# The pool of streamed weights at the upper end of SBUF, everything else 44 KB further down

## Chip, cores and metric

One core of one Trainium2 chip runs the whole program, a single launch. The metric is device time in microseconds, the median of several executions; one further execution is profiled, and all rows below come from it.

## What is computed

Three layers of a language model over 512 positions with a width of 1024, all in float32: an RWKV-7 layer, a layer of forgetting attention, and a layer that mixes sparse attention with a short convolution. Each is followed by an MLP. What takes most of the work are matrix products of activations and weights:

```python
def sq_relu_mlp(h, w_in, w_out):                       # 1024 -> 4096 -> 1024, three times
    return jnp.square(jax.nn.relu(h @ w_in)) @ w_out

def first_block(x, ...):
    for layer in range(DEPTH):                         # layer 0: RWKV-7, layer 1: forgetting attention
        ...
        x = x + rwkv7_time_mix(h, ...)                 # r, k, v, low-rank gates, a recurrence over 512 steps, w_o
        x = x + fox_layer(h, ...)                      # q, k, v projections, attention of 16 heads, w_o
        x = x + sq_relu_mlp(rmsnorm(x, mlp_norm_g[layer]), mlp_w_in[layer], mlp_w_out[layer])

def hybrid_layer(x, ...):                              # the third layer
    proj = xn @ w_in                                   # ... attention, convolution, gates ...
    x = x + mixed @ w_out
    return x + jnp.square(jax.nn.relu(h @ w_up)) @ w_down
```

## The kernel before

Activations lie feature-major: a tile holds 128 features by 512 positions, and eight tiles make a layer's width. To keep float32 accuracy each operand is split into a high part that TensorE reads as `fp32r` and a low part, the remainder: `wh` and `wl` for weights, `xg` and `xgl` (or `hid` and `hidl`, `xk` and `xkl`, and so on) for activations. Each block of 128 by 128 weights takes three matmuls: high with high, low with high, high with low.

Weights are streamed from DRAM by `load_w`: 512 KB at a time into a buffer `wr`, then ScalarE copies each 512 columns into `wh` (L95) and VectorE subtracts to get `wl` (L96). `wh` and `wl` have two buffers of 8 KB per partition each, `wr` three of 4 KB, so the pool `wp` has 44 KB per partition and lives as long as the program.

Two helpers run nearly all projections. `proj_fm` (L150, L151, L153; L156 where the low part is taken late) has a block of weights as the stationary operand, which TensorE loads, and 512 columns of activations as the moving one, which it streams through. `proj_tm` (L272 to L274) has it the other way round: 128 positions of activations stationary, 256 columns of weights moving. The three MLPs, the keys and receptances of the first layer, the convolution and the output projections use `proj_fm`; the values and the projections of the attention layers use `proj_tm`. L1459 to L1461 are the output projection of the first layer, with activations `O` stationary and weights `wo` moving.

What sets the order: every engine runs its instructions in the order that the program was built with, and a buffer is reused when its readers are done. Memory is handed out by pools in two stacks, one from the lower end of SBUF upward and one (`side="right"`) from the upper end downward; a pool starts where the one before it in its stack ends. The lower stack holds constants, `xall` (the residual stream), `wp`, and then the pools of the stage that runs: `net` with `xg` and `xgl`, and on top the pool of the MLP, of the attention and so on. Some of these begin with a block that nothing writes, made by `gap`: 1216 bytes in `fox`, 1728 in `nsa` and the second MLP, 640 in the third. The upper stack is used in the first layer alone: `rwk2` (with `xk`), `rwk1`, `rwk0`, later `rwk3`, `rwk7` and `rwk5`.

Of the kernel before, what the change touches and what calls it, by code (L numbers as in the profile page):

```python
# [31 lines left out]
class Net:  # L32
    def __init__(self, tc, a, ctx):
        self.tc, self.nc, self.a = tc, tc.nc, a
        nc = tc.nc
        nc.scalar.preload_act_table_set("exp_and_others")
        self.ctx = ctx
        self.cp = ctx.enter_context(tc.tile_pool(name="const", bufs=1))
        self.xp = ctx.enter_context(tc.tile_pool(name="xp", bufs=1))
        self.wp = ctx.enter_context(tc.tile_pool(name="wp", bufs=2))  # L40
        self.bs = ctx.enter_context(ExitStack())
        self.uid = 0
        self.nsc = 8
        self.set_banks(3, 2, 2, 1)
        cp = self.cp
        self.vec = cp.tile([P, len(VECS), NK], F32, name="vec")
        nc.sync.dma_start(self.vec, a["vecs"])
        self.ones = cp.tile([P, P], F32, name="ones")
        nc.gpsimd.memset(self.ones, 1.0)
        self.ident = cp.tile([P, P], F32, name="ident")  # L50
        nc.gpsimd.affine_select(self.ident, self.ones, pattern=[[-1, P]], compare_op=ALU.is_equal,
                                fill=0.0, base=0, channel_multiplier=1)
        self.xall = self.xp.tile([P, NK, T], F32, name="xall")
        self.xs = [self.xall[:, m, :] for m in range(NK)]
# [1628 lines left out]
```

## Time and profile before

| | us |
|---|---|
| median of 3 runs (lowest, highest) | 2290.26 (2289.51, 2296.22) |
| the profiled execution, its own time | 2293.3 |
| its span, first to last instruction | 2291.6 |
| TensorE busy | 2195.4 |
| VectorE, ScalarE, GpSimd busy | 1376.9, 937.2, 529.9 |

The first layer takes about the first 500 us of the span, the first MLP runs to about 840, forgetting attention to about 1090, the second MLP to about 1430, the third layer to about 1940 and the third MLP to the end. TensorE's record of a matmul lasts longer than the distance to the next one, since matmuls are pipelined; so the distance between the starts of two neighbours, called pitch below, says more than the length of one. The granted clock of a stretch is given as a share of the full 2.4 GHz.

### The profile page before, as it was taken

The page shows a single profiled execution, that of the slowest core. Times are in us where ns is not written, and L with a number is a line of the kernel's source. Part 1 is how long each engine was busy: PE and PEld are TensorE (multiplying, and loading weights), DVE is VectorE, ACT ScalarE, POOL GpSimd, SP SyncE. Part 2 cuts the span into 40 slices and gives each one's busy share as a digit, 9 for nine tenths or more (in the row PEclk, how much of TensorE's full clock was granted, in tenths as well). Part 3 has the DMA queues.
Part 4 walks back from the last instruction along what each step waited for, and adds up shares of the span by engine and source line. Part 5 has one row for each costly group of instructions (what it writes and reads, how often), then busy time and mean ns, then how long its engine had stood idle before and what let it go on. Part 6 is the DMA issues. An engine that isn't in the chain of part 4 may idle for free.

```text
span 2291.6 us, 32348 instructions
## 1 busy us (share of the span) xinstructions
PE 2195.4 (96%) x12161; PEld 1833.8 (80%) x12161; DVE 1376.9 (60%) x2750; ACT 937.2 (41%) x1920; POOL 529.9 (23%) x631
## 2 busy tenths in 40 slices
PE   4988868999999999999999999999999999999999
PEld 3768767878888889998788888898777788888887
DVE  8998778765444457776744444756665445444444
ACT  5575435433323345665523323344444333332331
POOL 5645211211121112444220120303331112012010
PEclk9999978999999999999999999999999999999999
DMA  3148634213322323332332223232223433223222
GB/s 121 42 136 253 187 85 137 93 48 102 101 92 92 105 98 103 102 101 72 108 101 100 92 92 108 78 111 84 90 85 107 134 111 111 92 93 105 97 92 83
DMA packets 104011, 237.32 MB, mean 104 GB/s; under 512 B 9664, under 2 KB 42176, under 8 KB 103856
## 3 DMA queue, kind: packets, MB, share of 16 engines
q1 hardware_dynamic: 82736, 220.58, 30.3%
q10 hardware_dynamic: 21120, 14.68, 2.1%
q8 instruction: 96, 1.57, 0.3%
q14 instruction: 59, 0.48, 0.1%
HBM read 210.02 MB, written 18.91 MB: 100 GB/s over the span
## 4 chain that ended last, share of the span: by engine, by line
PE 83%; DVE 9%; DMA 3%; ACT 2%; issue 1%; POOL 1%; SPq 0%; ACTq 0%; DVEq 0%; POOLq 0%
PE psacc L150 21%; PE psacc L151 21%; PE psacc L153 20%; PE psacc L272 2%; PE psacc L274 2%; PE psacc L273 2%; PE pso L384 2%; PE pst L374 1%; DVE wl L96 1%; DVE mix L1011 1%; DVE xgl L180 1%; PE pso L1459 1%; PE pso L1460 1%; PE pso L1461 1%; PE pso L1360 1%
## 5 line engine op out<-in xcount | busy, mean ns | idle before, releaser
L95 ACT CAST wh<-wr 128x512 fp32r<-128x512 f32 (+1 forms) x593 | 323.5, 616 | 448.4 <-PE psacc L153 322.6
L96 DVE TENSOR_TENSOR wl<-wr,wh 128x512 fp32r<-128x512 f32 (+1 forms) x581 | 421.8, 779 | 29.1 <-ACT wh L95 26.2
L153 PE MATMUL psacc<-xgl,wh 128*128 128x512 f32 x1104 | 431.7, 392 | 1.5 <-DVE xgl L180 1.5
L150 PE MATMUL psacc<-xg,wh 128*128 128x512 f32 x1104 | 432.6, 392 | 0.0
L151 PE MATMUL psacc<-xg,wl 128*128 128x512 f32 x1104 | 432.1, 391 | 0.0
L150 PE MATMUL psacc<-hid,wh 128*128 128x512 f32 x768 | 297.0, 389 | 0.0
L153 PE MATMUL psacc<-hidl,wh 128*128 128x512 f32 x768 | 297.0, 389 | 0.0
L151 PE MATMUL psacc<-hid,wl 128*128 128x512 f32 x768 | 296.8, 389 | 0.0
L260 POOL TENSOR_TENSOR xall<-xall,yt 128x512 f32<-128x512 f32 x72 | 106.9, 1484 | 663.2 <-DVE yt L259 663.2
L153 PEld LDWEIGHTS psacc<-xgl,wh 128*128 128x128 f32 x1104 | 207.3, 188 | 44.9 <-DVE xgl L180 3.0
L151 PEld LDWEIGHTS psacc<-xg,wl 128*128 128x128 f32 x1104 | 207.4, 188 | 42.5 <-issue 0.8
L150 PEld LDWEIGHTS psacc<-xg,wh 128*128 128x128 f32 x1104 | 207.4, 188 | 41.9 <-ACT xg L179 0.2
L259 DVE TENSOR_TENSOR yt<-psacc,rb 128x512 f32<-128x512 f32 x96 | 66.4, 692 | 265.6 <-PE psacc L153 265.6
L247 DVE TENSOR_TENSOR ht<-ht,psacc 128x512 f32<-128x512 f32 x96 | 66.0, 688 | 224.1 <-ACT ht L246 223.9
L246 ACT ACTIVATE ht<-psacc 128x512 f32<-128x512 f32 x96 | 57.4, 597 | 282.0 <-PE psacc L153 281.9
L153 PEld LDWEIGHTS psacc<-hidl,wh 128*128 128x128 f32 x768 | 144.2, 188 | 29.9
L151 PEld LDWEIGHTS psacc<-hid,wl 128*128 128x128 f32 x768 | 144.2, 188 | 29.8
L150 PEld LDWEIGHTS psacc<-hid,wh 128*128 128x128 f32 x768 | 144.2, 188 | 29.8
L272 PE MATMUL psacc<-wh,xg 128*128 128x256 f32 (+2 forms) x504 | 144.6, 287 | 2.6 <-ACT gt L659 1.5
L274 PE MATMUL psacc<-wh,xgl 128*128 128x256 f32 (+2 forms) x504 | 143.8, 286 | 0.6 <-DVE gq L605 0.6
L273 PE MATMUL psacc<-wl,xg 128*128 128x256 f32 (+2 forms) x504 | 143.7, 285 | 0.0
L204 POOL TENSOR_TENSOR ssacc<-ssacc,sq 128x512 f32<-128x512 f32 x35 | 53.0, 1513 | 224.7 <-ACT sq L203 223.8
(492 smaller groups left out, 3976.5 us busy)
## 6 DMA issues: line engine op xcount, KB each, us to landing
wr<-in_mlp_in_dram SPq DMA_DIRECT2D x96, 512.0 KB, 4.2
wr<-in_mlp_out_dram SPq DMA_DIRECT2D x96, 512.0 KB, 4.4
dQ<-q ACTq DMA_DIRECT2D x8, 1024.0 KB, 5.6
wr<-in_w_q_dram SPq DMA_DIRECT2D x12, 512.0 KB, 3.6
xall<-in_x_dram SPq DMA_DIRECT2D x16, 256.0 KB, 3.9
wr<-in_rw_k_dram SPq DMA_DIRECT2D x8, 512.0 KB, 3.5
wr<-in_rw_r_dram SPq DMA_DIRECT2D x8, 512.0 KB, 3.3
wr<-in_rw_v_dram SPq DMA_DIRECT2D x8, 512.0 KB, 4.6
```

What stands on the lines that cost most here:

```text
L95: nc.scalar.copy(h, r)
L96: (eng or nc.vector).tensor_tensor(wl[:rows, b:f], r, h.bitcast(F32), op=ALU.subtract)
L150: nc.tensor.matmul(ps_, wi[0], xh, start=i == 0, stop=False)
L151: nc.tensor.matmul(ps_, wi[1], xh, start=False, stop=False)
L153: nc.tensor.matmul(ps_, wi[0], xl, start=False, stop=i == n - 1)
L246: nc.scalar.activation(t, ps, AF.Relu)
L247: nc.vector.tensor_tensor(t, t, ps, op=ALU.mult)
L259: nc.vector.tensor_tensor(t, ps, r2, op=ALU.mult)
L260: (nc.vector if q == 3 else nc.gpsimd).tensor_tensor(self.xs[m], self.xs[m], t, op=ALU.add)
L272: nc.tensor.matmul(o, xh[:, b], wh, start=kt == 0, stop=False)
L273: nc.tensor.matmul(o, xh[:, b], wl, start=False, stop=False)
L274: nc.tensor.matmul(o, xl[:, b], wh, start=False, stop=kt == NK - 1)
```

## The change

```diff
         nc.scalar.preload_act_table_set("exp_and_others")
+        self.uid = 0
         self.ctx = ctx
         self.cp = ctx.enter_context(tc.tile_pool(name="const", bufs=1))
         self.xp = ctx.enter_context(tc.tile_pool(name="xp", bufs=1))
-        self.wp = ctx.enter_context(tc.tile_pool(name="wp", bufs=2))
+
+        self.gap(ctx.enter_context(tc.tile_pool(name="wpe", bufs=1, side="right")), 96)
+        self.wp = ctx.enter_context(tc.tile_pool(name="wp", bufs=2, side="right"))
         self.bs = ctx.enter_context(ExitStack())
-        self.uid = 0
```

`wp` goes from the lower stack to the upper one, above it a block of 96 bytes that nothing writes. All pools that stood on `wp` in the lower stack start 44 KB (45,056 bytes) lower, and the pools of the upper stack 45,152 bytes lower, since `wp` and the block now lie above them. Where the pools' first buffers lie in the built programs, in bytes of a partition, and the remainder by 256 of the buffers that TensorE reads:

| pool | starts at, before | after | buffers: remainder before, after |
|---|---|---|---|
| `wp` | 19,360 | 184,192 | `wh`, `wl`, `wr`: 160, 128 |
| `net` | 64,416 | 19,360 | `xg`, `xgl`: 160, 160 |
| first MLP | 121,504 | 76,448 | `hid`, `hidl`: 160, 160 |
| `rwk2` | 192,480 | 147,328 | `xk`, `xkl`: 224, 128 |
| `rwk5` | 163,520 | 118,368 | `O` (low part, last two blocks): 192, 96 |
| `rwkx` | 68,000 | 22,944 | `xr`, `xrl`: 160, 160 |

By 2048 bytes `xg` has a remainder of 928 and `hid` one of 672, before and after. `const` and `xp` stay where they are.

## Rows read from the trace of the kernel before

**Rows 1.** The page: busy time, share, instructions; then the chain that ended last.
```profile
PE 2195.4 (96%) x12161; PEld 1833.8 (80%) x12161; DVE 1376.9 (60%) x2750; ACT 937.2 (41%) x1920; POOL 529.9 (23%) x631
...
PE 83%; DVE 9%; DMA 3%; ACT 2%; issue 1%; POOL 1%; SPq 0%; ACTq 0%; DVEq 0%; POOLq 0%
PE psacc L150 21%; PE psacc L151 21%; PE psacc L153 20%; PE psacc L272 2%; PE psacc L274 2%; PE psacc L273 2%; PE pso L384 2%; PE pst L374 1%; DVE wl L96 1%; DVE mix L1011 1%; DVE xgl L180 1%; PE pso L1459 1%; PE pso L1460 1%; PE pso L1461 1%; PE pso L1360 1%
```

**Rows 2.** Stretches: length; busy (count) by PE, PEld, DVE, ACT, POOL; clock, DMA, GB/s.
```profile
600.00:800.00 200.00, 200.00 (x884) 165.62 (x883) 93.64 (x134) 64.44 (x118) 23.75 (x16) 1.00 0.30 96
...
2000.00:2200.00 200.00, 200.00 (x884) 165.58 (x884) 89.61 (x124) 57.14 (x105) 30.05 (x21) 1.00 0.29 97
```

**Rows 3.** Timeline of PE, first MLP: start, duration in us, line, output<-inputs.
```profile
600.21 0.39 PE L150 MATMUL psacc<-xg,wh 128*128 128x512 f32 x1
...
601.57 0.39 PE L150 MATMUL psacc<-xg,wh 128*128 128x512 f32 x1
```

**Rows 4.** Timeline of PE, keys of the first layer, first block.
```profile
38.52 0.40 PE L150 MATMUL psacc<-xk,wh 128*128 128x512 f32 x1
...
39.92 0.40 PE L150 MATMUL psacc<-xk,wh 128*128 128x512 f32 x1
```

**Rows 5.** Timeline of PE, keys of the first layer, last block.
```profile
86.23 0.39 PE L150 MATMUL psacc<-xk,wh 128*128 128x512 f32 x1
...
88.98 0.39 PE L150 MATMUL psacc<-xk,wh 128*128 128x512 f32 x1
```

**Rows 6.** Timeline of PE, output projection of the first layer.
```profile
479.76 0.39 PE L1461 MATMUL pso<-wo,O 128*128 128x512 f32 x1
...
481.16 0.39 PE L1461 MATMUL pso<-wo,O 128*128 128x512 f32 x1
```

**Rows 7.** Timeline of PE, values of the first layer, 256 columns.
```profile
191.39 0.28 PE L274 MATMUL psacc<-wh,xkl 128*128 128x256 f32 x1
...
192.07 0.28 PE L274 MATMUL psacc<-wh,xkl 128*128 128x256 f32 x1
```

**Rows 8.** Timeline of PE, values of the first layer, a later stretch.
```profile
224.74 0.28 PE L272 MATMUL psacc<-wh,xk 128*128 128x256 f32 x1
...
225.68 0.28 PE L274 MATMUL psacc<-wh,xkl 128*128 128x256 f32 x1
```

**Rows 9.** Timeline of PE, projections of the third layer, 256 columns.
```profile
1514.14 0.28 PE L273 MATMUL psacc<-wl,xg 128*128 128x256 f32 x1
...
1515.94 0.28 PE L273 MATMUL psacc<-wl,xg 128*128 128x256 f32 x1
```

**Rows 10.** Timeline of PE, first MLP, just after an interruption.
```profile
517.19 0.40 PE L151 MATMUL psacc<-xg,wl 128*128 128x512 f32 x1
...
519.27 0.39 PE L151 MATMUL psacc<-xg,wl 128*128 128x512 f32 x1
```

**Rows 11.** Instructions of L150 and L272: count, duration min/median/max in ns, first and last start.
```profile
L150 PE MATMUL psacc<-xg,wh x1104: 387/389/500, 498.0 to 2242.6; 128*128 128x512 f32 x184
L150 PE MATMUL psacc<-hid,wh x768: 389/389/476, 544.6 to 2286.1; 128*128 128x512 f32 x192
L150 PE MATMUL psacc<-xr,wh x64: 387/394/793, 97.7 to 161.5; 128*128 128x512 f32 x64
L150 PE MATMUL psacc<-oh,wh x64: 387/390/499, 1040.0 to 1106.0; 128*128 128x512 f32 x64
L150 PE MATMUL psacc<-zh,wh x64: 389/389/395, 1794.2 to 1886.9; 128*128 128x512 f32 x64
L150 PE MATMUL psacc<-mh,wh x64: 389/389/389, 1893.1 to 1935.9; 128*128 128x512 f32 x64
L150 PE MATMUL psacc<-noh,wh x32: 389/389/496, 1805.9 to 1892.4; 128*128 128x512 f32 x32
L272 PE MATMUL psacc<-wh,xg x504: 274/283/399, 849.8 to 1529.5; 128*128 128x256 f32 x149, 128*128 128x272 f32 x10, 128*128 128x280 f32 x9
L272 PE MATMUL psacc<-wh,xk x128: 276/281/469, 165.7 to 252.4; 128*128 128x256 f32 x128
```

## The prediction

> **What bounds the kernel now.** I read first the busy shares and the chain that ended last [rows 1]: TensorE is busy for 2195.4 of 2291.6 us (96%), and 83% of the chain is its own matmuls, most of them the three products of `proj_fm` (L150, L151, L153). So the time is, to a first approximation, the number of matmuls times the pitch from one start to the next. The second view is that pitch. Between 600 and 800 us, and again between 2000 and 2200 us, TensorE is busy without a gap at the full clock (1.00, which is 2.4 GHz) [rows 2]: 884 matmuls in 200 us, which with the 0.39 us that one matmul lasts is 200.39 / 884 = 226.7 ns each. The start times say the same: 600.21 to 601.57 us holds six pitches, 1.36 / 6 = 226.7 ns [rows 3]. 512 columns at 2.4 GHz are 213.3 ns, so each matmul carries 13.4 ns that isn't columns. Nothing waits there for VectorE, ScalarE or a DMA; only the pitch itself can make these stretches shorter or longer.
>
> **What the change moves.** No instruction is added, removed or reordered: the five engines have the same rows in the same order with the same waits (2353 buffers, 18,913 instructions in both). What changes is where buffers lie. I write places as the remainder of the start address by 256 bytes. Streamed weights (`wh`, `wl`, `wr`) go from 160 to 128. The buffers at the lower end (`xg`, `xgl`, `hid`, `hidl`, `oh`, `zh`, `mh`) keep 160, since 44 KB is a multiple of 256. The buffers at the upper end shift by 44 KB and 96 bytes: `xk` goes from 224 to 128. So in nearly all projections the two operands that TensorE reads, the stationary one (weights) and the moving one (activations), start at the same remainder before and 32 bytes apart after.
>
> **Does a remainder cost time?** The trace has pairs of both kinds, and the pitch differs between them at the same shape and the same full clock:
> Equal (160 and 160): 226.7 ns as above [rows 2, 3]. `xg` and `hid` differ by 256 bytes when taken by 2048, and both sit in these stretches, so I take 256 as the length that counts at most.
> 64 bytes apart (moving `xk` 224, stationary `wh` 160): 38.52 to 39.92 us holds six pitches, 1.40 / 6 = 233.3 ns, steady [rows 4]; a later stretch of the same pair, 86.23 to 88.98 us, has twelve, 2.75 / 12 = 229.2 ns, also steady [rows 5].
> 32 bytes apart in one of three (L1461, where `O`'s low part lies at 192 and the moving `wo` at 160, between two at 160 and 160): 479.76 to 481.16 us, six pitches, 1.40 / 6 = 233.3 ns [rows 6].
> Equal, but just after an interruption: 517.19 to 519.27 us, nine pitches, 2.08 / 9 = 231.1 ns [rows 10]; then it falls to 226.7 and stays. So 231 is what the pitch is while the two reads have not fallen into step, and the equal pair falls into a good step after about ten matmuls. The unequal pairs fall into 229.2 or 233.3.
> I read this as two streams of reads out of one memory that hold each other up now and then. That is argued from the pitches, not shown: these stretches also differ in what else runs beside them.
>
> **The sum.** Term 1, projections with weights stationary: L150 has 1104 + 768 + 64 + 64 + 64 + 64 + 32 = 2160 of them with moving operands at 160 [rows 11], and each has two companions (L151 with L153, or with L156 for `xr`), so 6480 matmuls go from equal to 32 bytes apart. Their new pitch isn't in the trace. Lower end of the loss: 32 bytes are nothing, 226.7 ns. Upper end: the worst steady pair, 233.3 ns. The rows show a step of 64 bytes at 229.2 to 233.3 and a mixture with 32 at 233.3; I take 230 ns, halfway between equal and the 64-byte step's worse value, since 32 is half of that distance. About one in ten of these matmuls stands just after an interruption and pays 231 already, so 6480 x 0.9 x 3.3 ns = +19 us (0 to +39).
> Term 2, the 256-column matmuls with weights moving (`proj_tm`, L272 to L274): here the equal pair isn't the good one. Equal, in the attention layers: 1514.14 to 1515.94 us, fifteen pitches, 1.80 / 15 = 120 ns [rows 9]. 64 bytes apart, with `xk` stationary: six pitches in 0.68 us, 113.3 ns [rows 7], or eight in 0.94 us, 117.5 ns [rows 8]. 3 x 504 = 1512 matmuls [rows 11] go from equal to 32 bytes apart; halfway to the middle of 113.3 and 117.5 (115.4) is 117.7, so 1512 x -2.3 ns = -3.5 us (-10 to 0).
> Term 3, the pairs that become equal: the 3 x 128 = 384 matmuls on `xk` in `rwkv_values` [rows 11] would go from about 115.4 to 120 ns, +1.8 us; the 192 of the keys (L150, L151, L156 on `xk`) from about 231 to 226.7, -0.8 us. Together +1 us (-1 to +2).
> Term 4, the other engines: the casts of the weights (L95, L96), VectorE, GpSimd and the loads also see new addresses. All buffers start at multiples of 32 bytes before and after, and in the long stretches TensorE never waits for them [rows 2]; the trace has no pair of placements to price it. I take 0 (-3 to +3); the recurrence of the first layer, where these engines are waited for, is where it would show.
> The sum is +19 - 3.5 + 1 + 0 = +16.5 us. The profiled execution took 2293.3 us (2291.6 span and 1.7 around it), 3.0 us over the median of the three runs, 2290.26; on the median the forecast is 2306.5, rounded 2306. Its own range is 2288 (term 1 costs nothing, the others as taken, -2.5 us) to 2331 (+39 and +2, term 2 nothing).
>
> **Rivals.**
> Nothing happens. What speaks for it: no wait, no instruction, no transfer changes, and the slow pitches that I blame on remainders stand in the interrupted stretches, where a matmul of another kind or shape is never far. Then the time is 2290 (2286 to 2294). The Trainium skill bears on this: "SBUF — State Buffer", section "Who interferes with whom", says that TensorE and ScalarE never wait for anybody at SBUF, and "TensorE: Matmul & The Clock Gate", section "Step-by-step: what each phase is for", that loading the next weights takes no read bandwidth from the running matmul, since TensorE has two read ports. By that rule addresses can't matter and this rival is right. The trace is against it as far as 226.7 and 233.3 ns for one shape at one clock go [rows 3, 4], but shows no cause.
> Faster. The equal pair isn't the floor: a 256-column matmul at 113.3 ns [rows 7] has 6.7 ns beyond its 106.7 ns of columns, where the 512-column one has 13.4. If the new distance of 32 bytes lets the long stretches fall into such a step, their pitch is 213.3 + 6.7 = 220.0 ns and term 1 becomes 6480 x 0.9 x -6.7 = -39 us; with term 2, -42 us: 2248. It decides itself in the first ten matmuls after each interruption: whichever step the reads fall into holds for the rest of the stretch. For it: with 256 columns every unequal pair is faster than the equal one. Against it: no stretch of 512 columns stays under 226.7 ns. A half of it (223 ns) gives 2270.
> The change doesn't do what it says: the buffers do lie where it puts them, and the order is the same, so this has no weight.
>
> **Chances and range.** Slower by the unequal pitch 0.50, of which 0.04 falls within 0.3%; nothing happens 0.17; faster 0.33, of which 0.01 falls within 0.3%. 0.3% (7 us) is about what a measurement of this kernel can tell from no change. So faster 0.32, same 0.22, slower 0.46. Cases of both signs hold much, so the range spans them: 2248 to 2331 with 0.2 left out, half below (220 ns or better in every stretch) and half above (233.3 ns or worse); the likeliest case's own range is 2288 to 2331.
>
> **What would show it.** In the profile after: the start times of L150, L151 and L153 in the middle of the first MLP (600 us), 230 ns apart if I am right, 226.7 if nothing happens, about 220 if it is faster; the same number in all three MLPs. L272 to L274 in the attention layers under 120 ns, on `xk` about 120. The keys' pitch at 38 us, now equal, down from 233.3 to 226.7 after some ten matmuls: this is the cleanest test of the reading, whatever the long stretches do. VectorE, ScalarE and GpSimd times per instruction unchanged within some ns. The forecast is wrong if 32 bytes act unlike half of 64, which no row excludes, or if the pitch hangs on what else reads the memory and not on the pair.

## The result

| | before | after |
|---|---|---|
| median (lowest, highest), us | 2291.89 (2289.51, 2296.22) | 2329.53 (2326.80, 2332.07) |
| executions | 4 | 4 |
| span of the profiled execution, us | 2291.6 | 2326.3 |
| ratio after / before | | 1.016, 95% interval 1.0147 to 1.0174 |

The change makes the kernel 37.6 us slower. The direction is the forecast's and the time lies in its range, at the upper end of the range of its likeliest case (2288 to 2331), but the forecast itself was +16 us, less than half of what came.

The page of the changed kernel (its code stands two lines further down, so L152, L153 and L155 are L150, L151 and L153 of before, and L274 to L276 are L272 to L274), busy time and then the chain, against [rows 1]:

```profile
PE 2230.8 (96%) x12161; PEld 1830.0 (79%) x12161; DVE 1378.4 (59%) x2750; ACT 937.3 (40%) x1920; POOL 531.1 (23%) x631
...
PE 83%; DVE 10%; DMA 3%; ACT 1%; issue 1%; POOL 1%; SPq 0%; ACTq 0%; DVEq 0%; POOLq 0%
PE psacc L152 21%; PE psacc L153 21%; PE psacc L155 21%; PE psacc L274 2%; PE psacc L276 2%; PE psacc L275 2%; PE pso L386 2%; PE pst L376 2%; DVE wl L98 1%; DVE mix L1013 1%; DMA Qe<-dQ 1%; PE pso L1461 1%; PE pso L1462 1%; PE pso L1463 1%; PE pss L1397 0%
```

The counts are the same, VectorE, ScalarE, GpSimd and the loading of weights (PEld) are within 4 us of before, and the chain has the same make-up. Only the matmuls' busy time grew, by 35.4 us (2195.4 to 2230.8), and the span by 34.7.

The stretches of 200 us in the first and the third MLP, columns as in [rows 2]:

```profile
600.00:800.00 200.00, 200.00 (x858) 160.61 (x857) 89.36 (x127) 61.43 (x112) 23.83 (x16) 1.00 0.29 95
2000.00:2200.00 200.00, 200.00 (x860) 160.69 (x859) 88.00 (x126) 59.03 (x108) 25.46 (x18) 1.00 0.29 95
```

TensorE is again busy without a gap at the full clock, and does 858 and 860 matmuls where it did 884: about 233 ns each in place of 226.7. What happened there is not a wait but a longer pitch, the same in both MLPs.

The timeline of TensorE in the changed kernel, six places, each by a first and a last row: the keys of the first layer just after the clock came up and some matmuls later, the values at two places, the first MLP just after an interruption and in its middle, and the projections of the third layer:

```profile
39.96 0.40 PE L153 MATMUL psacc<-xk,wl 128*128 128x512 f32 x1
...
42.04 0.39 PE L152 MATMUL psacc<-xk,wh 128*128 128x512 f32 x1
...
45.22 0.39 PE L153 MATMUL psacc<-xk,wl 128*128 128x512 f32 x1
...
47.26 0.39 PE L153 MATMUL psacc<-xk,wl 128*128 128x512 f32 x1
...
191.87 0.28 PE L274 MATMUL psacc<-wh,xk 128*128 128x256 f32 x1
...
192.59 0.28 PE L274 MATMUL psacc<-wh,xk 128*128 128x256 f32 x1
...
224.03 0.28 PE L276 MATMUL psacc<-wh,xkl 128*128 128x256 f32 x1
...
225.95 0.28 PE L274 MATMUL psacc<-wh,xk 128*128 128x256 f32 x1
...
519.11 0.39 PE L152 MATMUL psacc<-xg,wh 128*128 128x512 f32 x1
...
521.21 0.40 PE L152 MATMUL psacc<-xg,wh 128*128 128x512 f32 x1
...
599.80 0.39 PE L152 MATMUL psacc<-xg,wh 128*128 128x512 f32 x1
...
601.20 0.39 PE L152 MATMUL psacc<-xg,wh 128*128 128x512 f32 x1
...
1531.53 0.28 PE L274 MATMUL psacc<-wh,xg 128*128 128x256 f32 x1
...
1532.95 0.28 PE L274 MATMUL psacc<-wh,xg 128*128 128x256 f32 x1
```

Read by pairs, with the number of pitches between the two rows:

- Keys, now equal (128 and 128): nine pitches in 2.08 us, 231.1 ns, while the pair finds its step, and then nine in 2.04 us, 226.7 ns. Before it stood at 233.3 and, later, 229.2 [rows 4, 5]. The first nine take the 2.08 us that nine took after an interruption before [rows 10].
- Values, now equal: six pitches in 0.72 us and sixteen in 1.92 us, 120.0 ns both; before 113.3 and 117.5 [rows 7, 8].
- First MLP, now 32 bytes apart: nine pitches in 2.10 us just after an interruption, 233.3 ns, and six in 1.40 us in the middle, 233.3 ns; before 231.1 and 226.7 [rows 10, 3]. There is no better step into which this pair falls: in the whole trace no nine pitches of this kind in a row have a mean under 231.7 ns.
- Projections of the third layer, now 32 bytes apart: twelve pitches in 1.42 us, 118.3 ns; before 120 [rows 9].

Since both programs have the same 12,161 matmuls in the same order, the start of the same matmul can be compared in the two traces. By stages (from the first projection of one to that of the next; the first column begins with the first matmul of all, the last ends with the start of the last; us):

| | first layer | first MLP | forgetting attention | second MLP | third layer | third MLP |
|---|---|---|---|---|---|---|
| before | 485.2 | 351.8 | 257.1 | 350.9 | 478.9 | 350.0 |
| after | 486.4 | 360.3 | 255.8 | 360.6 | 485.5 | 359.9 |
| difference | +1.2 | +8.5 | -1.3 | +9.7 | +6.6 | +9.9 |

And by kind, each interval from one start to the next booked on the matmul that begins it, waits and all: the 6480 of term 1, without the very last, +36.7 us (1490.5 to 1527.2), the 1512 of term 2 -2.0 (190.3 to 188.3), values -0.1, keys +0.2, all else -0.2; together +34.6.

### The profile page after: what moved, and what is told of

The parts are those of the page before. It is cut to its first block, busy times and chain, and to the rows that moved or that the text cites. A ratio compares the mean times of both kernels' runs of the same rounds, so it can differ in the third digit from the quotient of the medians.

```text
span 2326.3 us, 32348 instructions
## 1 busy us (share of the span) xinstructions
PE 2230.8 (96%) x12161; PEld 1830.0 (79%) x12161; DVE 1378.4 (59%) x2750; ACT 937.3 (40%) x1920; POOL 531.1 (23%) x631
## 4 chain that ended last, share of the span: by engine, by line
PE 83%; DVE 10%; DMA 3%; ACT 1%; issue 1%; POOL 1%; SPq 0%; ACTq 0%; DVEq 0%; POOLq 0%
PE psacc L152 21%; PE psacc L153 21%; PE psacc L155 21%; PE psacc L274 2%; PE psacc L276 2%; PE psacc L275 2%; PE pso L386 2%; PE pst L376 2%; DVE wl L98 1%; DVE mix L1013 1%; DMA Qe<-dQ 1%; PE pso L1461 1%; PE pso L1462 1%; PE pso L1463 1%; PE pss L1397 0%
## 5 line engine op out<-in xcount | busy, mean ns | idle before, releaser
L152 PE MATMUL psacc<-xg,wh 128*128 128x512 f32 x1104 | 438.3, 397 | 0.0
L153 PE MATMUL psacc<-xg,wl 128*128 128x512 f32 x1104 | 437.8, 397 | 0.0
L155 PE MATMUL psacc<-xgl,wh 128*128 128x512 f32 x1104 | 437.1, 397 | 0.1
L152 PE MATMUL psacc<-hid,wh 128*128 128x512 f32 x768 | 301.6, 395 | 0.0
L155 PE MATMUL psacc<-hidl,wh 128*128 128x512 f32 x768 | 301.6, 395 | 0.0
L153 PE MATMUL psacc<-hid,wl 128*128 128x512 f32 x768 | 301.4, 395 | 0.0
L155 PEld LDWEIGHTS psacc<-xgl,wh 128*128 128x128 f32 x1104 | 207.0, 188 | 49.4 <-DVE xgl L182 1.0
L153 PEld LDWEIGHTS psacc<-xg,wl 128*128 128x128 f32 x1104 | 207.2, 188 | 48.7 <-issue 0.8
L152 PEld LDWEIGHTS psacc<-xg,wh 128*128 128x128 f32 x1104 | 207.2, 188 | 48.1 <-ACT xg L181 0.2
L155 PEld LDWEIGHTS psacc<-hidl,wh 128*128 128x128 f32 x768 | 143.9, 187 | 35.3
L152 PEld LDWEIGHTS psacc<-hid,wh 128*128 128x128 f32 x768 | 144.0, 187 | 35.1
L153 PEld LDWEIGHTS psacc<-hid,wl 128*128 128x128 f32 x768 | 144.0, 187 | 35.0
L274 PE MATMUL psacc<-wh,xg 128*128 128x256 f32 (+2 forms) x504 | 144.0, 286 | 2.6 <-ACT gt L661 1.4
L276 PE MATMUL psacc<-wh,xgl 128*128 128x256 f32 (+2 forms) x504 | 143.1, 284 | 0.6 <-DVE gq L607 0.6
```

Of the source, the lines that this page charges most:

```text
L152: nc.tensor.matmul(ps_, wi[0], xh, start=i == 0, stop=False)
L153: nc.tensor.matmul(ps_, wi[1], xh, start=False, stop=False)
L155: nc.tensor.matmul(ps_, wi[0], xl, start=False, stop=i == n - 1)
L274: nc.tensor.matmul(o, xh[:, b], wh, start=kt == 0, stop=False)
L276: nc.tensor.matmul(o, xl[:, b], wh, start=False, stop=kt == NK - 1)
```

## The experiments

The theory: the distance by 256 bytes between the start addresses of a matmul's stationary and moving operand sets the pitch. Rivals: the place of the weights at the upper end costs something by itself; or the pitch hangs on what else reads the memory at the time.

### The upper end without the distance

```diff
-        self.gap(ctx.enter_context(tc.tile_pool(name="wpe", bufs=1, side="right")), 96)
+        self.gap(ctx.enter_context(tc.tile_pool(name="wpe", bufs=1, side="right")), 64)
```

> The changed kernel with a block of 64 bytes instead of 96 above the weights: weights at the upper end as in the change, but at a remainder of 160 like the activations. Theory A (the distance by 256 of the two operands' start addresses sets the pitch): 226.7 ns in the long stretches, 2288 to 2293 us, as before the change. Theory B (the place counts: weights at the upper end, far from the activations): 233.3 ns and 2327 to 2332 us, as after the change.

Measured: 2293.83 us against 2292.68, ratio 1.0007 (0.9996 to 1.0017). The stretch from 600 to 800 us of this kernel:

```profile
600.00:800.00 200.00, 200.00 (x884) 165.60 (x883) 91.30 (x130) 62.53 (x114) 23.78 (x16) 1.00 0.30 98
```

884 matmuls again. 32 bytes less above the pool give the whole loss back, so neither the upper end nor the move of everything else by 44 KB costs anything that can be told.

### The distance without the upper end

```diff
+        self.uid = 0
+        self.gap(ctx.enter_context(tc.tile_pool(name="wpe", bufs=1)), 224)
         self.wp = ctx.enter_context(tc.tile_pool(name="wp", bufs=2))
+        self.gap(ctx.enter_context(tc.tile_pool(name="wpf", bufs=1)), 32)
```

> The kernel before, weights in the lower stack as ever, with an unwritten block of 224 bytes ahead of them and one of 32 behind: weights at a remainder of 128, all that stands on them 256 bytes higher and so at 160 as before, the upper stack untouched. Theory A: 233.3 ns in the long stretches and 2326 to 2334 us. Theory B: 226.7 ns and 2288 to 2293 us.

Measured: 2327.97 us, ratio 1.0155 (1.0137 to 1.0172). The same stretch:

```profile
600.00:800.00 200.00, 200.00 (x858) 160.61 (x858) 89.26 (x127) 61.40 (x112) 23.83 (x16) 1.00 0.29 95
```

The kernel before, with its weights 32 bytes off and nothing else of the change, loses what the change loses. The two runs together settle which part of the change acts.

### Other distances

The changed kernel with no block above the pool (stationary operand 64 bytes after the moving one), and with 128 bytes (64 bytes before it):

```diff
-        self.gap(ctx.enter_context(tc.tile_pool(name="wpe", bufs=1, side="right")), 96)
```

> The changed kernel without the block of 96 bytes: weights at a remainder of 224, 64 bytes above the activations' 160. Theory A: slower than before the change, long stretches at 229 to 234 ns (233.3 or 229.2 are the settled values that a 64-byte distance had in the kernel before), 2303 to 2332 us; the attention projections of 256 columns at 113 to 118 ns. Theory B: as after the change, 2327 to 2332 us, with 120 ns.

```diff
-        self.gap(ctx.enter_context(tc.tile_pool(name="wpe", bufs=1, side="right")), 96)
+        self.gap(ctx.enter_context(tc.tile_pool(name="wpe", bufs=1, side="right")), 128)
```

> The changed kernel with 128 bytes instead of 96 above the pool of weights: weights at a remainder of 96, activations of the long stretches at 160, so the stationary operand lies 64 bytes before the moving one. Theory (the distance of the pair by 256 bytes sets the pitch, as in the series of matmuls alone): 229 ns there, so 6480 matmuls go from a mean of 227.25 to about 229.2 (+13 us), the attention layers' 256-column matmuls get a distance of +64 (117.8 ns, -2.6 us): 2302 us, ratio 1.0045. Rival, that any unequal pair costs what 32 bytes cost: 2329 us. Rival, that it is the weights' own place (remainder 96 or 128, neither at 160) that costs: 2329 us.

Measured: 64 after, 2327.0 us in a single execution; 64 before, 2298.97 us, ratio 1.0029 (1.0014 to 1.0043). The stretch from 600 to 800 us, first of the one, then of the other:

```profile
600.00:800.00 200.00, 200.00 (x858) 161.13 (x858) 89.94 (x128) 61.54 (x112) 23.76 (x16) 1.00 0.29 95
```

```profile
600.00:800.00 200.00, 200.00 (x875) 164.10 (x874) 91.09 (x130) 62.47 (x114) 23.77 (x16) 1.00 0.30 97
```

64 bytes after cost as much as 32 before. By its time that run can't tell its two theories apart, since 2327 lies in the range of both; its 256-column matmuls can: 117.3 ns on the mean in the forgetting attention, not the 120 of theory B. 64 bytes before cost 200.39 / 875 = 229.0 ns, as forecast from the series of matmuls below, and the time is far from 2329: unequal pairs are not all alike, and weights that left 160 do not cost by themselves. The run came out 3 us under its expectation. The attention layers can account for it: their 256-column matmuls had a mean pitch of 115.5 ns in the forgetting attention and 114.2 in the third layer (neighbours under 140 ns apart, 921 and 279 of them), not the 117.8 of the series, which is 1152 x 2.3 + 360 x 3.6 = 3.9 us. The two steps that this distance had before, 113.3 and 117.5 [rows 7, 8], are seen here too, twelve pitches in 1.36 and in 1.41 us:

```profile
866.02 0.28 PE L276 MATMUL psacc<-wh,xgl 128*128 128x256 f32 x1
...
867.38 0.28 PE L276 MATMUL psacc<-wh,xgl 128*128 128x256 f32 x1
...
887.06 0.28 PE L276 MATMUL psacc<-wh,xgl 128*128 128x256 f32 x1
...
888.47 0.28 PE L276 MATMUL psacc<-wh,xgl 128*128 128x256 f32 x1
```

What chooses between them stays open.

### Matmuls alone

Each series is 60 matmuls on one pair of places, one series after the other:

```python
for c, (n, m, s) in enumerate(CASES):          # columns, remainder of moving, of stationary
    for k in range(N):
        o, q = (k % 16) * 256 + s // 4, (k // 2 % (3584 // n)) * n + m // 4
        nc.tensor.matmul(ps[:, :n], w[:, o:o + 128], x[:, q:q + n], start=k == 0, stop=k == N - 1)
```

> Leaves the whole computation out: a block of weights and a block of activations, and 27 series of 60 matmuls each of equal shape, with nothing else running; only the remainders of the two start addresses by 256 differ from series to series. Theory A: the series settle as in the kernel: 512 columns, 226.7 ns at 160 and 160, 233.3 ns at 160 and 128, between 226 and 234 at the others; 256 columns, 120 ns at 160 and 160, 118.3 at 128 and 160, 113.3 or 117.8 at 160 and 224. Rival C (the pitch comes from other engines' accesses): one pitch for all series of a shape, 226.7 ns or less.

The stretch with all series but the first three, and then the timeline with a row for each series (start, duration, name, count):

```profile
50.00:330.00 280.00, 268.17 (x1450) 230.68 (x1448) 3.95 (x25) 0.00 (x0) 0.00 (x0) 0.99 0.02 8
```

```profile
52.07 14.15 PE L134 MATMUL casead<-x,w 128*128 128x512 f32 x60
66.06 14.16 PE L134 MATMUL caseae<-x,w 128*128 128x512 f32 x60
...
136.04 13.91 PE L134 MATMUL casebd<-x,w 128*128 128x512 f32 x60
149.78 14.07 PE L134 MATMUL casebe<-x,w 128*128 128x512 f32 x60
...
177.69 13.79 PE L134 MATMUL caseca<-x,w 128*128 128x512 f32 x60
191.31 13.79 PE L134 MATMUL casecb<-x,w 128*128 128x512 f32 x60
204.95 14.15 PE L134 MATMUL casecc<-x,w 128*128 128x512 f32 x60
218.94 14.16 PE L134 MATMUL casecd<-x,w 128*128 128x512 f32 x60
...
246.87 7.36 PE L134 MATMUL casecf<-x,w 128*128 128x256 f32 x60
254.06 7.26 PE L134 MATMUL caseda<-x,w 128*128 128x256 f32 x60
261.16 7.23 PE L134 MATMUL casedb<-x,w 128*128 128x256 f32 x60
268.23 7.20 PE L134 MATMUL casedc<-x,w 128*128 128x256 f32 x60
275.27 7.28 PE L134 MATMUL casedd<-x,w 128*128 128x256 f32 x60
```

From the start of one series to that of the next there are 60 pitches. `casead` (moving 160, stationary 192) takes 66.06 - 52.07 = 13.99 us, 233.2 ns. `casebd` (160, 96) has 229.0, `caseca` (160, 144) 227.0, `casecb` (128, 128) 227.3 with its first matmuls, `casecc` (128, 160) 233.2. The settled pitch, over the last 24 of each series (the first three, which give the values at 0 and 16 for 512 columns, begin interleaved, but the last 50 matmuls of each run alone):

| stationary minus moving, bytes | 0 | 16 | 32 | 48 | 64 | 96 | 128 | 160 | 192 (-64) | 208 | 224 (-32) | 240 (-16) |
|---|---|---|---|---|---|---|---|---|---|---|---|---|
| 512 columns, ns | 226.7 | 226.7 | 233.3 | 233.3 | 233.3 | 234.3 | 232.1 | 233.3 | 228.9 | 232.0 | 233.3 | 226.7 |
| 256 columns, ns | 120.0 | | 118.3 | | 117.8 | 117.3 | 118.6 | 120.0 | 117.8 | | 117.8 | |

In this stretch ScalarE and GpSimd do nothing, VectorE 3.95 us in 280, the DMAs 2%. The pitches of the two kernels stand here all the same: 226.7 and 233.3 for the long stretches, 120.0 and 118.3 (`casecf` 7.19 us, `caseda` 7.10 us for 60) for the attention layers. So the rival that something else reads the memory at the time is out: TensorE's own two operands are enough.

A second set asked whether only the distance counts. The list of pairs is all that differs:

> As the series of matmuls alone before (26 series of 60; nearly all of the reference's computation is left out). First, equal pairs at other places: 160, 160, 0, 4, 16, 32, 64, 224 by 256 bytes, 512 columns. Theory (only the distance counts): 226.7 ns in all. Rival (an absolute place counts): some differ. Then the stationary operand 8, 12, 20, 24, -4, -8, -12, -20, -24 bytes from the moving one. A distance of 16 gave 226.7 and 4 gave 232.3, 32 gave 233.3. If a grid of 16 bytes counts: all about 232 to 233. If it is the size of the distance: 8 and 12 at 226.7 to 232. Then 256, 512, 768 bytes: theory 226.7 in all. Then 256 columns at distances of 16, -16, 8, 80, 112, 256: between 117 and 120 ns; under 117 would be a better place than any seen.

```profile
52.43 14.35 PE L134 MATMUL casead<-x,w 128*128 128x512 f32 x60
66.62 14.03 PE L134 MATMUL caseae<-x,w 128*128 128x512 f32 x60
80.49 13.77 PE L134 MATMUL caseaf<-x,w 128*128 128x512 f32 x60
94.10 13.80 PE L134 MATMUL caseba<-x,w 128*128 128x512 f32 x60
...
260.26 13.76 PE L134 MATMUL caseda<-x,w 128*128 128x512 f32 x60
273.86 13.76 PE L134 MATMUL casedb<-x,w 128*128 128x512 f32 x60
...
301.60 7.10 PE L134 MATMUL casede<-x,w 128*128 128x256 f32 x60
308.53 7.36 PE L134 MATMUL casedf<-x,w 128*128 128x256 f32 x60
```

Equal pairs at 0, 32, 64, 160 and 224 settle at 226.7 ns (`caseaf`, 32 and 32: 13.61 us for 60, 226.8), and so do distances of 256, 512 (`caseda`: 13.60 us) and 768 bytes. But equal pairs at 16 and 4 have 231.2 (`caseae`: 13.87 us) and 236.5 ns (`casead`: 14.19 us). So "only the distance counts" holds for starts at multiples of 32 bytes, as all these starts in the kernels before and after are, and not below. Small distances from 160 give no plain rule: 8 bytes 230.7, 12 bytes 230.0, 20 to 24 bytes 233.3 and 231.1, and backward 4, 8 and 12 bytes 233.3 each. With 256 columns a distance of 8 (`casede`) is the best seen in a series, 6.93 us for 60, 115.5 ns.

### A version with each kind at its better distance

The 512-column projections are faster with an equal pair, the 256-column ones with an unequal one at most distances, and both use the same pool of weights. In the forgetting attention alone the stationary activations can be moved. Three distances were run, with an equal one as the control:

```diff
-    def gained(self, gain=None):
+    def gained(self, gain=None, o=0):
...
-            h = self.np.tile([P, T], F32R, tag="xg", bufs=NK, name=self.nm("xg"))
-            l = self.np.tile([P, T], F32R, tag="xgl", bufs=NK, name=self.nm("xgl"))
+            h, l = (t[:, o + kt * T:o + kt * T + T] for t in self.xt)
...
-            st, X = {}, self.gained()
+            st, X = {}, self.gained(o=16)
...
+        n.xt = [n.np.tile([P, NK * T + 64], F32R, name=nm) for nm in ("xg", "xgl")]
```

with `o` of 0, 24, 16 and 2 elements of 4 bytes.

> Control for the next one. The kernel before, with the eight xg tiles as slices of one tile and the eight xgl tiles too, each with 256 bytes more at its end; everything above lies 512 bytes higher, remainders as before. All theories: no change, 2292 us, pitch 226.7 ns and 120 ns as before.

> As the one before, but in the forgetting attention alone the xg and xgl slices start 96 bytes later, so that the stationary activations there lie 96 bytes after the moving weights (256 columns); all pairs with 512 columns stay equal. Theory: 1152 matmuls go from a mean of 119.5 to 117.3 ns, -2.5 us, ratio 0.999, and this would be faster than both kernels; the long stretches stay at 226.7 ns. Rival, that 256-column matmuls in the kernel are bound by something else there: no change.

> As the run with 96 bytes in the forgetting attention, but 64: stationary activations at 224, moving weights at 160, 512-column pairs equal as before. With the weights 64 bytes down (weights 96, activations 160, the same distance) these matmuls had a mean pitch of 115.4 ns; alone, at 224 and 160, they had 117.8. Theory A (in the kernel the distance of 64 gives 115.4 wherever the pair lies): 1152 x (115.4 - 119.4) = -4.6 us, 2287.5, ratio 0.998. Theory B (the place counts too, 117.8 at 160): 1152 x -1.6 = -1.9 us, 2290, not told from before.

> The same with 8 bytes: stationary activations at 168, moving weights at 160. Alone this pair had 115.5 ns against 120.0 for the equal one. Theory: 1152 x (115.5 - 119.4) = -4.5 us, 2287.5, ratio 0.998, unless ScalarE and VectorE, which write these tiles, are slower at 8 bytes. Rival: no gain, since something else in that stage ends last: 2292.

| distance there | mean pitch, ns | stage, us | median, us | ratio (95% interval) |
|---|---|---|---|---|
| 0 (control) | 119.4 | 260.0 | 2292.26 | 1.0011 (1.0000 to 1.0021) |
| 96 | 118.1 | 257.7 | 2291.29 | 0.9993 (0.9983 to 1.0003) |
| 64 | 114.8 | 252.3 | 2290.30 | 0.9986 (0.9977 to 0.9996) |
| 8 | 116.4 | 254.5 | 2289.95 | 0.9992 (0.9982 to 1.0002) |

The mean pitch is taken over those under 140 ns between neighbours of that kind in the stage, 912 to 921 of them. The runs with 0 and 96 are compared with executions of the kernel before with a median of 2292.23 us, those with 64 and 8 with others of 2293.21. Two rows of the timeline of the kernel with 64 bytes:

```profile
889.78 0.28 PE L271 MATMUL psacc<-wh,xg 128*128 128x256 f32 x1
...
891.60 0.28 PE L272 MATMUL psacc<-wl,xg 128*128 128x256 f32 x1
```

Sixteen pitches in 1.82 us, 113.8 ns. With 64 bytes theory A of that run holds (114.8 ns on the mean, 115.4 expected), and its kernel comes out faster than both: 0.14% under before, with an interval that excludes 1 and nothing to spare. As the best of three that were tried, it is a hint and not a proof. 96 and 8 bytes lower the pitch too, 96 by half of what was expected, but their times are not told from before's. The stage itself is no finer measure: it took 257.1 us before and 260.0 in the control, with the same pitches, so a part of what it varies by is not the pitch.

## Why the prediction was right in direction and short in size

**The bound.** Right: TensorE's pitch is the time. Nothing else moved by more than 4 us of busy time.

**The reading that the pair of addresses sets the pitch.** Right, and now shown: it was argued from pitches that stood beside other work, and the series of matmuls alone give the same numbers with next to nothing beside them. Its "cleanest test" came out as written: the keys fell from 233.3 to 226.7 ns after nine pitches at 231.1.

**Term 1, the step that failed.** It put +19 us; these matmuls took +36.7. What failed is the pitch of 230 ns. It came from "32 is half of that distance": a straight line was drawn between 0 and 64 bytes. The measured curve has no such line. It stays at 226.7 for 16 bytes to either side and is at 233.3 at 32, 48 and 64; the value at 64 backward is lower (228.9) than at 32 backward (233.3). The prediction named this as a way to be wrong, and had 233.3 as its upper end: with that the same sum, its factor of 0.9 included, is 6480 x 0.9 x 6.6 = +38.5 us, 2 us from the measured +36.7 (5.7 ns for each). A row in hand pointed that way: L1459 to L1461, one pair in three at 32 bytes, had 233.3 on the mean of the three [rows 6], and I ranked it below the halving. It did not settle it, being a mixture: with the two equal pairs at 226.7 the third would have had 246, which no series shows. The factor of 0.9 was near the mark: of the pitches of this kind under 260 ns, 14% are among the first nine of an unbroken stretch. But I took those as paying the same in any case, and on the mean they went from 230.3 to 232.9; the later ones went from 226.7 to 233.3.

**Term 2.** Right in sign, too large: -2.0 us by the intervals with their waits, against -3.5. The undisturbed pitches agree: from 119.4 and 119.9 to 118.3 in both layers, about -1.2 ns x 1512 = -1.8 us. I had 117.7.

**Term 3.** The pitches came as written (values 120.0, keys 226.7), the sum of +1 us did not: values -0.1, keys +0.2 with their waits. The 384 values take 58 us with their waits, where 384 pitches of 120 ns are 46 us; a pitch that grows or shrinks there can be made up by the wait behind it. That it was is argued and not shown.

**Term 4.** Right: VectorE 1376.9 to 1378.4, ScalarE 937.2 to 937.3, GpSimd 529.9 to 531.1 us; the first layer +1.2 us, less than it differs by among the profiles of these kernels (480.2 to 486.6 us).

**Nothing happens.** Out. The Trainium skill, "TensorE: Matmul & The Clock Gate", section "Step-by-step: what each phase is for", has the load of the next weights take no read bandwidth from the running matmul. What the prediction drew from it, that addresses can't matter, does not hold here: with TensorE alone at work, the two addresses move the pitch from 226.7 to 233.3 ns. Whether it is the load that takes the time, no run shows. What the Trainium skill says in "SBUF — State Buffer", section "Who interferes with whom", that TensorE never waits for another engine, agrees with these runs as far as they go: the pitches are the same with the other engines at work and without.

**Faster.** Out for 512 columns: none of the 37 series of 512 columns settles under 226.6 ns, so the 220 that I carried over from the 256-column rows was seen at no distance tried. It had a third of the chance and held the lower end of the range; the argument against it, that no stretch in the trace had ever been faster than 226.7, was the better one.

**What stays open.** Why the curve has this form. That the reads of the two operands meet somewhere in the memory fits, but no run here shows where, nor why 256 columns want a distance that 512 do not, nor why the same distance has two steps at 256 columns, and in the keys of before at 512 (233.3 and 229.2 [rows 4, 5]).

## To carry to other kernels

When a kernel is bound by TensorE and streams weights, the remainder by 256 bytes of where a pool starts is a tuning knob like any other: print the start addresses of the stationary and the moving operand for each kind of matmul and compare the pitch of pairs in the trace, before a pool is moved or a few bytes of padding are put in. Here a 32-byte slip cost 1.6%. And where no row has the distance in question by itself, don't draw a line between two others: a row that holds it among others is a better guide, and a short series of matmuls at that distance better still.

## What the runs showed of the hardware

- With fp32r operands and new weights for every matmul, 512 columns at the full clock take 226.7 ns from start to start if stationary and moving operand start at the same remainder by 256 bytes (at multiples of 32), and 228.9 to 234.3 at other multiples of 32; 256 columns take 120.0 ns at an equal remainder, and 117.3 to 118.6 at most others in the series of matmuls alone, 114.8 on the mean in the attention with 64 bytes between.
- In the kernel an equal pair of 512 columns finds its step within about nine matmuls after an interruption (up to 231.9 ns on the mean over them) and then keeps it until the next (226.7 over all later ones). In the series alone some equal pairs had it from the start (32 and 32: 226.8 over all 60).
- Equal remainders that are not multiples of 32 bytes are worse: 231.2 ns at 16, 236.5 at 4.
